# Small float32 matmuls of a hybrid decoder's mixer, regrouped over the tiles of the PE array

## Chip, cores and metric

One core of a Trainium2 chip runs the whole program. The metric is device time in microseconds, the median of the runs shown; less is better. One launch computes one layer for 512 prompt tokens and for 8 requests of 4 new tokens each, 544 tokens together.

## What is computed

The reference is one layer of a decoder in float32: a half-step feed-forward network with layer norm, a mixer, layer norm, and a second half-step network with layer norm. The change lies in the mixer. Its projection `h = x @ w_in` is split into an attention group of 8 heads (dilated windows, for the sampled tokens over a cache of 512 positions) and a delta group of 8 heads (short convolution, then the gated delta rule in chunks of 64 tokens). Cut to what matters here:

```
a     = where(strict, (kb @ k.T) * decay, 0)       # per head and chunk
t_inv = inverse(eye + a)                           # unit lower triangular
u     = t_inv @ (v * beta);   w = t_inv @ (kb * exp(gc))
intra = where(tril, (q @ k.T) * decay, 0)
def step(s, ...):                                  # 8 chunks, one after the other
    v_new = u_i - w_i @ s
    o_i   = qd_i @ s + intra_i @ v_new
    s     = s * gl_i + kd_i.T @ v_new
```

The attention of the prompt is `softmax(q k.T + bias) @ v` over causal blocks of 128 tokens. The sampled tokens have the same delta rule with one chunk of 4 tokens per request, and each request's state is updated as above.

## The kernel before

The two feed-forward networks are dense products of 128 by 128 weights with 272 token columns, kept in two float32r parts (tiles `wh`, `wl`, or `g` where weights lie there). They are outside the change. Between them stands the mixer, whose pieces are generators that yield what they want next (an engine, a rough duration, PSUM banks, tile slots). The class `Weave` runs them as lanes: it takes the lane that can start first by its own table of durations, so the numbers in each `yield` set the order in which instructions are written. Dense projection products are lanes marked `PE*`; they fill in between the small ones. PE, DVE, ACT, POOL and the DMA queue of SP each run their instructions in the order written, and wait on semaphores. The tile framework may still move an instruction by its priority, unless `together` (a chain in which each matmul is tied behind the last, the first waits for everything that the set reads or overwrites) holds it.

A float32 matmul of 64 columns is two matmul instructions in the trace, so a set of 16 calls of `mm` shows as x32. All `mm` calls have line 309. An operand on partitions 0 to 63 or 64 to 127 uses the upper or lower half of the PE array's rows, an output there its left or right columns: a 64 by 64 product occupies one of four array tiles, and one on 32 partitions a smaller tile. The pieces that the change touches, with heads in four pairs `j`, two heads `hp` in each, and chunks `u`, `p2`:

- `pair(j)`, from line 1246: k k.T and k q.T of all chunks, 32 products, into two banks `pa[hp]`.
- `inverse_load`, `solve(j)` (line 1368, one lane for each j): two sets of 32 by 32 products (`py`, `pz`) complete the inverse. Between them an ACT copy (line 1388) and after them a DVE copy (line 1398). Then 16 products for `u` (`pu`), 16 for `w` (`pw`), each set with a `yield` and an ACT copy of its own.
- `recurrence`, from line 1449: for each of 8 chunks 16 products with the state `ST` (w and q: `pb`), a DVE subtraction (line 1474), 8 products `pk` with KD, a DVE addition that makes the next state (line 1483). `chunk_out` (line 1489) then does 8 products `pi` with IN in a step of its own, two DVE multiplications (line 1502) and one DVE addition (line 1506).
- `state_sample`, line 1718: four sets of 16 products, one for each j, one bank at a time.
- `values`, line 1815: for each j and half of the prompt, two query blocks `qb`, each a set of its own behind the probabilities of its block.

In `pb`, the order of the loops is w first, then q:

```
for w, rows in ((WT, r), (QT, ro)):
    for j in range(4):
        for hp in range(2):
            mm(pb[hp][rows, j * 64:j * 64 + 64], w[j][rh, i * 64:i * 64 + 64], ST[rh, j])
```

Cached keys and values of the sampled tokens (lines 1860, 1888), biases (1774), `w_out` (2022) and the residual (2043) are loaded by SP's queue, in the order written, into tile slots that the mixer's other work frees.

Of the kernel before, what the change touches and what calls it, by code (L numbers as in the profile page):

```python
# [16 lines left out]
ALU = mybir.AluOpType  # L17
# [193 lines left out]
def trunk(ctx, tc, slots, x_prompt, x_sample, cache_k, cache_v, state_gdn, state_conv, rel_bias,  # L211
# [1003 lines left out]
    def pair(j):  # L1215
# [30 lines left out]
        for u in range(4):  # L1246
            for p2 in range(2):
                for hp in range(2):
                    c0 = u * 128 + p2 * 64
                    l = k[64 * hp:64 * hp + 64, c0:c0 + 64]  # L1250
                    o = pa[hp][64 * p2:64 * p2 + 64]
                    mm(o[:, u * 64:u * 64 + 64], l, l)
                    mm(o[:, 256 + u * 64:256 + u * 64 + 64], l, q[64 * hp:64 * hp + 64, c0:c0 + 64])
# [87 lines left out]
    XI = {}  # L1341

    def inverse_load():
# [6 lines left out]
        for i in range(4):  # L1350
            WT[i] = wj[:, i]
            XI[i] = xs_[i // 2][:, (i % 2) * 256:(i % 2) * 256 + 256]
# [15 lines left out]
    def solve(j):  # L1368

        yield "wait", "inverse loaded"  # L1370
        yield "wait", ("scaled", j)
        tt = WT[j]
        tv = tt.rearrange("p (n c) -> p n c", n=8)
        xv = XI[j].rearrange("p (n c) -> p n c", n=8)
        av = A21[j // 2][:, (j % 2) * 256:(j % 2) * 256 + 256].rearrange("p (n c) -> p n c", n=8)
        yield "PE", 0.6, 1
# [8 lines left out]
        yield "ACT", 0.7, [py]  # L1385
        for p2 in range(2):
            r = slice(64 * p2 + 32, 64 * p2 + 64)
            S.activation(xv[r], py[r, :256].rearrange("p (n c) -> p n c", n=8), AF.Copy, scale=-1.0)
        yield "PE", 0.6, 1
        pz = wv.bank()  # L1390
        for n in range(8):
# [3 lines left out]
        yield "DVE", 0.7, [pz]  # L1395
        for p2 in range(2):
            r = slice(64 * p2, 64 * p2 + 32)
            V.tensor_copy(tv[r, :, 32:64], pz[r, :256].rearrange("p (n c) -> p n c", n=8))
        yield "PE", 1.3, 1
        pu = wv.bank()  # L1400
        for u in range(4):
            for hp in range(2):
                c0 = u * 128 + hp * 64
                for p2 in range(2):
                    r = slice(64 * p2, 64 * p2 + 64)
                    mm(pu[r, c0:c0 + 64], tt[r, c0:c0 + 64], VU[r, j, c0:c0 + 64])
        yield "ACT", 0.8, [pu]
        S.copy(VU[:, j], pu)
        yield "PE", 1.3, 2
        pw = [wv.bank(), wv.bank()]  # L1410
        for u in range(4):
            for hp in range(2):
                c0 = u * 128 + hp * 64
                for p2 in range(2):
                    r = slice(64 * p2, 64 * p2 + 64)
                    mm(pw[p2][64 * hp:64 * hp + 64, u * 64:u * 64 + 64], KG[j][r, c0:c0 + 64], tt[r, c0:c0 + 64])
        w4 = WT[j].rearrange("p (u a c) -> p u a c", u=4, a=2)
        for p2 in range(2):
            yield "ACT", 0.35, [pw[p2]]
            S.copy(w4[:, :, p2], pw[p2][:, :256].rearrange("p (u c) -> p u c", u=4))  # L1420
        wv.post(("solved", j))
        yield "G", -1
# [25 lines left out]
    def recurrence():  # L1448
# [5 lines left out]
        for u in range(4):  # L1454
            ou = G(512)
            ov = ou.rearrange("p (j t e) -> p j t e", j=4, t=2)
            for p2 in range(2):
# [5 lines left out]
                for w, rows in ((WT, r), (QT, ro)):  # L1463
                    for j in range(4):
# [11 lines left out]
                yield "PE", 0.7, 2  # L1476
                pk, pi = wv.bank(), wv.bank()
                for j in range(4):
                    for hp in range(2):
                        c0 = u * 128 + hp * 64  # L1480
                        mm(pk[64 * hp:64 * hp + 64, j * 64:j * 64 + 64], KD[j][r, c0:c0 + 64], vv[r, j, hp])
# [9 lines left out]
    def chunk_out(u, p2, vv, pb, pi, ov):  # L1491
# [3 lines left out]
        yield "PE", 0.7  # L1495
        for j in range(4):
            for hp in range(2):
                c0 = u * 128 + hp * 64
                mm(pi[ro, (2 * j + hp) * 64:(2 * j + hp) * 64 + 64], IN[j][r, c0:c0 + 64], vv[r, j, hp])
# [5 lines left out]
        yield "DVE", 0.65, [pi]  # L1505
        V.tensor_tensor(ou[ro], pi[ro], ou[ro], op=ALU.add)
# [191 lines left out]
    def state_sample(kd, vn, sts):  # L1698
# [19 lines left out]
        for j in range(4):  # L1718
            r = slice(32 * j, 32 * j + 32)
            yield "PE", 0.9, 1  # L1720
            pk = wv.bank()
            for bp in range(4):
                for hp in range(2):
                    for b2 in range(2):
                        c0 = (2 * bp + hp) * 64
                        mm(pk[64 * b2:64 * b2 + 64, c0:c0 + 64], kd[r, hp * 64:hp * 64 + 64],
                           vms[bp // 2][r, 2 * (bp % 2) + b2, hp * 64:hp * 64 + 64])
            for bp in range(4):
                yield ("DVE", 0.25) if bp < 3 else ("DVE", 0.25, [pk])
                sj = sts[bp][:, 2 * j:2 * j + 2]  # L1730
                V.tensor_tensor(sj, pk[:, 128 * bp:128 * bp + 128].rearrange("p (t e) -> p t e", t=2), sj, op=ALU.add)
# [489 lines left out]
```

## Time and profile before

| | before |
|---|---|
| median of 3 runs | 1218.44 us (1215.99 to 1218.8) |
| the profiled execution | 1218.54 us, span of instructions 1216.8 us |
| PE matmul busy | 1167.1 us, 96% of the span |
| DVE busy | 905.4 us, 74% |
| ACT busy | 515.8 us, 42% |
| POOL busy | 288.0 us, 24% |
| granted PE clock, mean | 0.977 |
| chain that ended last | PE 77%, of it line 309 73%; DVE 10%; DMA 4% |

The chain names what the last instruction waited for, step by step back to the start; three quarters of it are matmuls of line 309, dense and small together. Busy shares are means over stages that are limited by different things, so the rows further below are taken stage by stage. In them a matmul's own duration includes the time that it spends behind others in the pipeline: what a set costs is read from the start of its first instruction to the start of the next group's.

### The profile page before, as it was taken

What the parts mean: (1) busy time and instruction counts of PE and PEld (TensorE: products, weight loads), DVE (VectorE), ACT (ScalarE), POOL (GpSimd) and SP (SyncE); (2) the same over time, 40 slices, a digit from 0 to 9 for tenths busy, and PEclk for the clock granted to TensorE, in tenths of its full rate; (3) what the DMA queues carried; (4) which work ended last, traced back from release to release, by engine and by line L of the source; (5) the groups of instructions that cost most, each with busy time, mean ns of one, the idle gap of its engine ahead of it and who ended that gap; (6) DMA issues with size and microseconds to landing.
All of it is one profiled execution on the core that took longest, in us unless ns stands there. A gap on an engine that the chain in (4) does not pass through costs nothing.

```text
span 1216.8 us, 25657 instructions
## 1 busy us (share of the span) xinstructions
PE 1167.1 (96%) x10375; PEld 1104.9 (91%) x10375; DVE 905.4 (74%) x1905; ACT 515.8 (42%) x1035; POOL 288.0 (24%) x363
## 2 busy tenths in 40 slices
PE   8899999999999999999999999988999999999994
PEld 7899999999999888999888675877999999999994
DVE  6878887877766587794366647688988777777767
ACT  6444444343444465433411544456444444444432
POOL 2321121111100047961314100033211111111003
PEclk8999999999999999999999999989999999999997
DMA  7553323322233222336104995321322324242112
GB/s 169 152 174 97 115 88 108 105 73 87 70 97 121 75 69 78 97 91 159 58 13 124 322 299 191 114 77 46 113 92 73 98 79 122 87 122 70 56 50 74
DMA packets 165442, 130.91 MB, mean 108 GB/s; under 512 B 31758, under 2 KB 152100, under 8 KB 165324
## 3 DMA queue, kind: packets, MB, share of 16 engines
q1 hardware_dynamic: 163852, 124.82, 34.3%
q0 software_dynamic: 1472, 4.46, 1.2%
q8 instruction: 81, 1.33, 0.5%
q14 instruction: 37, 0.30, 0.1%
HBM read 119.63 MB, written 12.33 MB: 108 GB/s over the span
## 4 chain that ended last, share of the span: by engine, by line
PE 77%; DVE 10%; DMA 4%; POOL 3%; ACT 2%; SPq 2%; issue 2%; DVEq 0%; POOLq 0%; ACTq 0%
PE bank L309 73%; PE bank L525 1%; PE bank L1866 1%; DVE wl L313 1%; DMA wf<-in_ffn_w_gate 1%; DMA wf<-in_ffn_w_up 1%; DMA g<-in_cache_attn_k 1%; PE bank L582 1%; DVE wf L1333 1%; PE bank L1812 1%; DVE tmp L1331 1%; DVE wl L923 1%; DVE lna L504 1%; DVE g L313 1%; DVE g L1001 1%
## 5 line engine op out<-in xcount | busy, mean ns | idle before, releaser
L309 PE MATMUL bank<-g,wh 128*128 128x272 f32 (+2 forms) x4864 | 943.5, 292 | 11.9 <-DVE g L313 7.0
L309 PEld LDWEIGHTS bank<-g,wh 128*128 128x128 f32 x4864 | 769.4, 190 | 24.5 <-DVE g L313 7.6
L309 PE MATMUL bank<-g,wl 128*128 128x272 f32 (+2 forms) x2432 | 703.6, 290 | 0.0
L309 PEld LDWEIGHTS bank<-g,wl 128*128 128x128 f32 x2432 | 460.8, 190 | 3.6 <-issue 3.2
L312 ACT CAST wh<-wf 128x512 fp32r<-128x512 f32 (+2 forms) x176 | 111.7, 648 | 138.8 <-PE bank L309 113.0
L712 POOL TENSOR_TENSOR wf<-wf 128x512 f32<-128x512 f32 x40 | 63.7, 1592 | 360.5 <-DVE vu L710 344.9
L313 DVE TENSOR_TENSOR wl<-wf,wh 128x512 fp32r<-128x512 f32 (+2 forms) x172 | 135.6, 799 | 11.1 <-ACT wh L312 9.0
L309 PE MATMUL bank<-g 64*64 64x64 f32 (+15 forms) x1708 | 128.7, 295 | 3.7 <-DVE g L1596 2.4
L309 PEld LDWEIGHTS bank<-g 64*64 64x64 f32 (+7 forms) x1708 | 89.8, 142 | 23.2 <-issue 10.7
L312 ACT CAST wh<-vu 128x512 fp32r<-128x512 f32 x120 | 72.3, 618 | 70.7 <-PE bank L309 70.0
L713 POOL TENSOR_TENSOR vu<-wf,vu 128x512 f32<-128x512 f32 x40 | 59.7, 1493 | 125.4 <-DVE wl L313 121.1
L313 DVE TENSOR_TENSOR wl<-vu,wh 128x512 fp32r<-128x512 f32 x120 | 81.5, 693 | 10.4 <-ACT wh L312 6.2
L313 DVE TENSOR_TENSOR g<-g 128x544 fp32r<-128x544 f32 (+1 forms) x80 | 71.4, 919 | 0.0
L312 ACT CAST wh<-g 128x512 fp32r<-128x512 f32 x64 | 38.0, 618 | 59.5 <-issue 42.0
L312 ACT CAST g<-g 128x544 fp32r<-128x544 f32 (+1 forms) x80 | 44.3, 582 | 39.6 <-DVE g L755 24.0
L313 DVE TENSOR_TENSOR wl<-g,wh 128x512 fp32r<-128x512 f32 x64 | 43.0, 693 | 24.2 <-ACT wh L312 23.4
L887 ACT COPY g<-bank 128x512 f32<-128x512 f32 (+4 forms) x64 | 30.3, 501 | 60.0 <-PE bank L309 21.6
L923 DVE TENSOR_TENSOR wl<-wf,wh 128x1024 fp32r<-128x1024 f32 x28 | 37.7, 1348 | 20.6 <-ACT wh L921 20.4
L775 DVE TENSOR_TENSOR g<-bank,g 128x272 f32<-128x272 f32 x96 | 40.0, 431 | 12.5 <-PE bank L309 12.4
L711 DVE TENSOR_TENSOR vu<-vu,wf 128x512 f32<-128x512 f32 x40 | 47.6, 1190 | 1.8
L710 DVE TENSOR_TENSOR vu<-wf 128x512 f32<-128x512 f32 x40 | 27.5, 689 | 20.9 <-DMA wf<-in_ffn_w_gate 18.3
L921 ACT CAST wh<-wf 128x1024 fp32r<-128x1024 f32 x28 | 29.2, 1050 | 28.0 <-PE bank L309 14.0
(313 smaller groups left out, 1116.7 us busy)
## 6 DMA issues: line engine op xcount, KB each, us to landing
wf<-in_ffn_w_gate SPq DMA_DIRECT2D x21, 1024.0 KB
wf<-in_ffn_w_up SPq DMA_DIRECT2D x21, 1024.0 KB
g<-in_ffn_w_down SPq DMA_DIRECT2D x64, 256.0 KB
wf<-in_w_in SPq DMA_DIRECT2D x14, 1024.0 KB
g<-in_cache_attn_k SPq DMA_DIRECT2D x32, 256.0 KB
g<-in_cache_attn_v SPq DMA_DIRECT2D x32, 256.0 KB
wf<-in_ffn_w_down SPq DMA_DIRECT2D x8, 768.0 KB
wf<-in_w_out SPq DMA_DIRECT2D x4, 1024.0 KB
```

The lines of the kernel that those rows point to most:

```text
L309: return PE.matmul(out, l, r, start=start, stop=stop, skip_group_check=again)
L312: S.copy(h, f)
L313: (GP if pool else V).tensor_tensor(l, f, h.bitcast(F32), op=ALU.subtract)
L504: V.tensor_mul(a, y, y)
L710: V.tensor_add(s1, a21, a22)
L711: V.tensor_sub(s2, s1, a11)
L712: GP.tensor_tensor(a21, a11, a21, op=ALU.subtract)
L713: GP.tensor_tensor(s4, a12, s2, op=ALU.subtract)
L775: V.tensor_add(r, pd, r)
L887: return S.copy(out, src)
L921: S.copy(h, fm)
L923: V.tensor_sub(l, fm, h.bitcast(F32))
```

## The change

Each piece keeps its products; their order and their grouping move. In `pair`, the k k.T and k q.T products no longer alternate on the same tile. `solve` takes two pairs j at once: 32 products in `py`, 32 in `pz`, with one copy of twice the width behind each, and `u` and `w` of one j form one chained set. In the recurrence, w and q products alternate, and `pi` moves out of `chunk_out` into one chained set behind `pk`; its outputs for hp = 1 go to the other half of the partitions, so that the addition in `chunk_out` becomes two of half the width. `state_sample` takes two j at once, in two banks. `values` chains both query blocks in one set, and waits for the probabilities of both.

```
@@ pair
-            for p2 in range(2):
-                for hp in range(2):
-                    ...
-                    mm(o[:, u * 64:u * 64 + 64], l, l)
-                    mm(o[:, 256 + u * 64:256 + u * 64 + 64], l, q[64 * hp:64 * hp + 64, c0:c0 + 64])
+            for i, m in enumerate((k, q)):
+                for p2 in range(2):
+                    for hp in range(2):
+                        ...
+                        mm(pa[hp][64 * p2:64 * p2 + 64, 256 * i + u * 64:256 * i + u * 64 + 64], k[rh, c0:c0 + 64], m[rh, c0:c0 + 64])
@@ solve
-    def solve(j):
+    def solve(j0):
...
-        for n in range(8):
+        for n in range(16):
             for p2 in range(2):
...
-        yield "PE", 1.3, 1
-        pu = wv.bank()
...
-        yield "PE", 1.3, 2
-        pw = [wv.bank(), wv.bank()]
...
+        for j in js:
+            tt = WT[j]
+            yield "PE", 1.5, 3
+            pu, pw = wv.bank(), [wv.bank(), wv.bank()]
+            ...
+            together([(pu[r, c0:c0 + 64], tt[r, c0:c0 + 64], VU[r, j, c0:c0 + 64]) for u, hp, p2, c0, r in at] +
+                     [(pw[p2][64 * hp:64 * hp + 64, u * 64:u * 64 + 64], KG[j][r, c0:c0 + 64], tt[r, c0:c0 + 64])
+                      for u, hp, p2, c0, r in at])
@@ recurrence
-                for w, rows in ((WT, r), (QT, ro)):
-                    for j in range(4):
+                for j in range(4):
+                    for w, rows in ((WT, r), (QT, ro)):
                         for hp in range(2):
...
-                yield "PE", 0.7, 2
+                yield "PE", 1.0, 2
                 pk, pi = wv.bank(), wv.bank()
-                for j in range(4):
-                    for hp in range(2):
-                        c0 = u * 128 + hp * 64
-                        mm(pk[64 * hp:64 * hp + 64, j * 64:j * 64 + 64], KD[j][r, c0:c0 + 64], vv[r, j, hp])
+                together([(pk[64 * hp:64 * hp + 64, j * 64:j * 64 + 64], KD[j][r, of(j, hp)], vv[r, j, hp])
+                          for j in range(4) for hp in range(2)] +
+                         [(pi[(ro, r)[hp], (2 * j + hp) * 64:(2 * j + hp) * 64 + 64], IN[j][r, of(j, hp)], vv[r, j, hp])
+                          for j in range(4) for hp in range(2)])
@@ chunk_out
-        yield "PE", 0.7
-        for j in range(4):
-            for hp in range(2):
-                c0 = u * 128 + hp * 64
-                mm(pi[ro, (2 * j + hp) * 64:(2 * j + hp) * 64 + 64], IN[j][r, c0:c0 + 64], vv[r, j, hp])
...
-        V.tensor_tensor(ou[ro], pi[ro], ou[ro], op=ALU.add)
+        for hp in range(2):
+            V.tensor_tensor(ov[ro, :, hp], pv[(ro, r)[hp], :, hp], ov[ro, :, hp], op=ALU.add)
@@ state_sample
-        for j in range(4):
-            ...
-            pk = wv.bank()
+        for js in ((0, 1), (2, 3)):
+            yield "PE", 1.0, 2
+            pk = {j: wv.bank() for j in js}
...
+                        for j in js:
+                            r = slice(32 * j, 32 * j + 32)
+                            c0 = (2 * bp + hp) * 64
+                            mm(pk[j][64 * b2:64 * b2 + 64, c0:c0 + 64], kd[r, hp * 64:hp * 64 + 64],
+                               vms[bp // 2][r, 2 * (bp % 2) + b2, hp * 64:hp * 64 + 64])
@@ values
-                    if qb == qs[0]:
-                        yield "PE", 0.2 * (qb + 1), 1
-                        po = wv.bank()
-                    else:
-                        yield "PE", 0.2 * (qb + 1)
-                    together([... for kb in range(qb + 1) for hp in (1, 0)])
-                    yield "G", -2
+                yield "PE", 0.2 * sum(qb + 1 for qb in qs), 1
+                po = wv.bank()
+                together([... for qb in qs for kb in range(qb + 1) for hp in (1, 0)])
+                yield "G", -4
```

The order of PE in the solves. Names: 32x32 with `g` alone is `py`, with `wf` is `pz` (the inverse lies in a `wf` buffer), `vu,wf` is `pu`, `wh` and `wl` are dense products. Before:

```order
L309 MATMUL bank<-g 32x32 x16
L309 MATMUL bank<-wf_7088,g 32x32 x16
L309 MATMUL bank<-g,wh 128x288 x2
L309 MATMUL bank<-g,wl 128x288
L309 MATMUL bank<-g,wh 128x288 x2
L309 MATMUL bank<-g,wl 128x288
L309 MATMUL bank<-wf_7088,g 32x32 x16
```

and with the change:

```order
L309 MATMUL bank<-g 32x32 x32
L309 MATMUL bank<-g,wh 128x288 x2
L309 MATMUL bank<-g,wl 128x288
L309 MATMUL bank<-g,wh 128x288 x2
L309 MATMUL bank<-g,wl 128x288
L309 MATMUL bank<-wf_7088,g 32x32 x32
```

Two pairs now share a set, and a set stands alone between dense products half as often.

The order of PE in the first step of the recurrence; `g 64x64` holds `pk`, `pi` and the sampled states. Before, a dense product has slipped between the first and the other seven products of `pk`, and `pi` comes five dense products later:

```order
L309 MATMUL bank<-g 64x64
L309 MATMUL bank<-g,wh 128x256
L309 MATMUL bank<-g 64x64 x7
L964 MATMUL bank<-cst,g 128x128 x4
L309 MATMUL bank<-g,wh 128x256
L309 MATMUL bank<-g,wl 128x256
L309 MATMUL bank<-g,wh 128x256 x2
L309 MATMUL bank<-g,wl 128x256
L309 MATMUL bank<-g 64x64 x8
```

With the change `pk` and `pi` are the x16, and the x32 is the first set of the sampled states, four tiles in two banks:

```order
L309 MATMUL bank<-g 64x64 x16
L1664 MATMUL bank<-cst,g 128x128
L309 MATMUL bank<-g,wh 128x288
L309 MATMUL bank<-g,wl 128x288
L309 MATMUL bank<-g 64x64 x32
```

The second set of the sampled states does not stay whole: the scheduler puts its j = 2 products first (7, then 9 behind the next `pk` and `pi`) and all 16 of j = 3 behind the fourth state set.

The order of PE at the seventh and eighth step, where cached keys are transposed on line 1866 (1857 with the change). Before:

```order
L309 MATMUL bank<-state,wf_7088 64x64 x8
L309 MATMUL bank<-state,g 64x64 x8
L1866 MATMUL bank<-cst,g 128x128 x4
L1529 MATMUL bank<-cst,g 128x128 x4
L309 MATMUL bank<-g,wl 128x256
L309 MATMUL bank<-g,wh 128x256 x2
L309 MATMUL bank<-g,wl 128x256
L309 MATMUL bank<-g 64x64 x16
```

and with the change, from the end of the seventh state set:

```order
L309 MATMUL bank<-state,g 64x64 x2
L1857 MATMUL bank<-cst,g 128x128 x4
L309 MATMUL bank<-g 64x64 x16
L309 MATMUL bank<-state,wf_7088 64x64 x2
L309 MATMUL bank<-state,g 64x64 x2
```

Here only four transposes stand between a state set and the `pk` that needs its subtraction, and nothing between `pk`, `pi` and the eighth state set.

Over the whole order of PE, the solves come in 13 stretches of small matmuls before and 8 with the change, the recurrence with the sampled states in 27 and 16, the attention of prompt and samples in 27 and 22 (a stretch ends where full-array work, a dense product or a transpose, follows). The number of matmuls is the same.

## Rows read from the trace of the kernel before

**Rows 1.** Stretches: length, busy PE, PEld, DVE, ACT, POOL, clock, DMA share, GB/s.

```profile
560.00:662.00 102.00, 101.62 (x1724) 92.38 (x1723) 53.19 (x180) 25.21 (x50) 27.57 (x50) 1.00 0.27 68
662.00:700.00 38.00, 34.98 (x311) 25.97 (x311) 26.08 (x89) 20.67 (x44) 5.33 (x9) 0.96 0.93 292
700.00:740.00 40.00, 38.42 (x344) 30.46 (x343) 21.78 (x47) 14.26 (x28) 0.71 (x4) 1.00 0.79 254
740.00:770.00 30.00, 27.77 (x210) 15.90 (x211) 23.69 (x102) 15.88 (x53) 0.00 (x0) 0.89 0.73 234
```

**Rows 2.** Timeline of PE, solves: a set of pu, a set of pw.

```profile
577.28 0.29 PE L309 MATMUL bank<-g,wl 128*128 128x288 f32 x1
577.50 1.15 PE L309 MATMUL bank<-vu,wf 64*64 64x64 f32 x32
578.58 0.50 PE L309 MATMUL bank<-g,wh 128*128 128x256 f32 x2
578.92 0.28 PE L309 MATMUL bank<-g,wl 128*128 128x256 f32 x1
579.04 0.40 PE L309 MATMUL bank<-g,wh 128*128 128x256 f32 x2
579.28 0.27 PE L309 MATMUL bank<-g,wl 128*128 128x256 f32 x1
579.48 0.69 PE L309 MATMUL bank<-wf,g 64*64 64x64 f32 x32
580.11 0.50 PE L309 MATMUL bank<-g,wh 128*128 128x256 f32 x2
```

**Rows 3.** Timeline of PE, pk (14 of 16) and pi of the first step.

```profile
604.88 0.68 PE L309 MATMUL bank<-g 64*64 64x64 f32 x14
605.48 0.66 PE L964 MATMUL bank<-cst,g 128*128 128x128 f32 x4
...
606.66 1.14 PE L309 MATMUL bank<-g 64*64 64x64 f32 x16
607.74 0.50 PE L309 MATMUL bank<-g,wh 128*128 128x256 f32 x2
```

**Rows 4.** Timeline of PE, first state set of the recurrence.

```profile
600.35 0.51 PE L309 MATMUL bank<-state,wf 64*64 64x64 f32 x10
...
600.82 0.51 PE L309 MATMUL bank<-state,g 64*64 64x64 f32 x11
601.26 0.53 PE L309 MATMUL bank<-g,wh 128*128 128x288 f32 x2
```

**Rows 5.** Groups of PE by form, 560 to 662: sampled states.

```profile
L309 PE MATMUL bank<-g 32*64 32x64 f32 x128 | 5.1, 222 | 0.0
```

**Rows 6.** Timeline of PE, a set of pair: start, length, line, operands, count.

```profile
462.18 1.30 PE L309 MATMUL bank<-g 64*64 64x64 f32 x64
463.41 0.51 PE L309 MATMUL bank<-g,wh 128*128 128x256 f32 x2
```

**Rows 7.** Groups of DVE, 560 to 670: the addition and the reduction of chunk_out.

```profile
L1506 DVE TENSOR_TENSOR g<-bank,g 64x512 f32<-64x512 f32 x8 | 5.5, 687 | 8.9 <-PE bank L309 8.8
L1514 DVE TENSOR_REDUCE oss<-g 128x8 f32<-128x512 f32 x4 | 2.7, 687 | 1.9 <-ACT g L1511 1.9
```

**Rows 8.** Timeline of DVE, subtractions of the eighth step.

```profile
660.98 0.42 DVE L1474 TENSOR_TENSOR g<-vu,bank 64x256 f32<-64x256 f32 x1 [2.58 <-PE bank L309]
...
661.89 0.42 DVE L1474 TENSOR_TENSOR g<-vu,bank 64x256 f32<-64x256 f32 x1
```

**Rows 9.** Waits of PE, 660 to 770: who for whom, us, times, longest.

```profile
PE bank L1866 <- DMA g<-in_cache_attn_k: 2.5, 2, 1.7
```

**Rows 10.** Waits of SP's queue, 430 to 860.

```profile
SPq L1860 <- PE bank L309: 54.1, 5, 44.2
```

**Rows 11.** Timeline of PE, transposes of probabilities and the waits before them.

```profile
757.85 0.55 PE L1812 MATMUL bank<-cst,g 128*128 128x128 f32 x3 [1.63 <-DVE g L1807]
758.76 0.48 PE L1812 MATMUL bank<-cst,g 128*128 128x128 f32 x1 [0.36 <-DVE sm L1797]
```

More of the change, by code (lines that the diff above doesn't have):

```diff
@@ L1351, in inverse_load @@
             WT[i] = wj[:, i]
-            XI[i] = xs_[i // 2][:, (i % 2) * 256:(i % 2) * 256 + 256]
+            XI[i] = xs_[i // 2]
+        WJ.append(wj)
         for p2 in range(2):
@@ L1384, in solve @@
                     after(i, first)
-        yield "ACT", 0.7, [py]
+        yield "ACT", 1.1, [py]
         for p2 in range(2):
             r = slice(64 * p2 + 32, 64 * p2 + 64)
-            S.activation(xv[r], py[r, :256].rearrange("p (n c) -> p n c", n=8), AF.Copy, scale=-1.0)
-        yield "PE", 0.6, 1
+            S.activation(xv[r], py[r].rearrange("p (n c) -> p n c", n=16), AF.Copy, scale=-1.0)
+        yield "PE", 1.0, 1
         pz = wv.bank()
-        for n in range(8):
+        for n in range(16):
             for p2 in range(2):
@@ L1394, in solve @@
                 mm(pz[64 * p2:64 * p2 + 32, n * 32:n * 32 + 32], xv[r, n], tv[r, n, 32:64])
-        yield "DVE", 0.7, [pz]
+        yield "DVE", 1.2, [pz]
         for p2 in range(2):
             r = slice(64 * p2, 64 * p2 + 32)
-            V.tensor_copy(tv[r, :, 32:64], pz[r, :256].rearrange("p (n c) -> p n c", n=8))
-        yield "PE", 1.3, 1
-        pu = wv.bank()
-        for u in range(4):
-            for hp in range(2):
-                c0 = u * 128 + hp * 64
[L1404 to L1408, printed above, removed]
-        yield "PE", 1.3, 2
-        pw = [wv.bank(), wv.bank()]
-        for u in range(4):
-            for hp in range(2):
-                c0 = u * 128 + hp * 64
[L1414 to L1422, printed above, removed]
+            V.tensor_copy(tv[r, :, 32:64], pz[r].rearrange("p (n c) -> p n c", n=16))
+        for j in js:
+            tt = WT[j]
+            yield "PE", 1.5, 3
+            pu, pw = wv.bank(), [wv.bank(), wv.bank()]
+            at = [(u, hp, p2, u * 128 + hp * 64, slice(64 * p2, 64 * p2 + 64)) for u in range(4) for hp in range(2) for p2 in range(2)]
+            together([(pu[r, c0:c0 + 64], tt[r, c0:c0 + 64], VU[r, j, c0:c0 + 64]) for u, hp, p2, c0, r in at] +
+                     [(pw[p2][64 * hp:64 * hp + 64, u * 64:u * 64 + 64], KG[j][r, c0:c0 + 64], tt[r, c0:c0 + 64])
+                      for u, hp, p2, c0, r in at])
+            yield "ACT", 0.6, [pu]
+            S.copy(VU[:, j], pu)
+            w4 = WT[j].rearrange("p (u a c) -> p u a c", u=4, a=2)
+            for p2 in range(2):
+                yield "ACT", 0.35, [pw[p2]]
+                S.copy(w4[:, :, p2], pw[p2][:, :256].rearrange("p (u c) -> p u c", u=4))
+            wv.post(("solved", j))
+            yield "G", -1
     def keep(kind, i):
@@ L1724, in state_sample @@
                     for b2 in range(2):
[L1725 to L1731, printed above, removed]
+                        for j in js:
+                            r = slice(32 * j, 32 * j + 32)
+                            c0 = (2 * bp + hp) * 64
+                            mm(pk[j][64 * b2:64 * b2 + 64, c0:c0 + 64], kd[r, hp * 64:hp * 64 + 64],
+                               vms[bp // 2][r, 2 * (bp % 2) + b2, hp * 64:hp * 64 + 64])
+            for j in js:
+                for bp in range(4):
+                    yield ("DVE", 0.25) if bp < 3 else ("DVE", 0.25, [pk[j]])
+                    sj = sts[bp][:, 2 * j:2 * j + 2]
+                    V.tensor_tensor(sj, pk[j][:, 128 * bp:128 * bp + 128].rearrange("p (t e) -> p t e", t=2), sj, op=ALU.add)
         for b in range(8):
@@ L2108, in trunk @@
     wv.add(gates(), recurrence())
-    for j in range(4):
+    for j in (0, 2):
         wv.add(solve(j))
```

35 lines of the change are left out of this document (15 added, 20 removed).

## The prediction

> **What bounds the kernel now.** I read the windows first: is PE the limit in the stages that the change touches, or something beside it? From 560 to 662 us, where solves, recurrence and sampled states run among dense products, PE is busy for 101.62 of 102 us at full clock, DVE for 53.19, and DMA moves little (0.27) [rows 1]. A microsecond taken from PE there is a microsecond off the time, as long as no wait takes its place. From 662 to 740 us, where attention begins, PE still has 73.4 of 78 us, but DMA is at 0.93 and then 0.79; from 740 to 770 the clock is 0.89 and PE idles for 2.2 us [rows 1]. So the question is whether what is saved ahead of 662 us survives the next hundred. The dense products of the two networks behind and ahead are untouched.
>
> Next the timeline of PE, set by set, since a matmul's own duration includes its place in the pipeline. I take differences of starts. A set of `pw`, which goes round four tiles, holds 32 instructions and takes 0.63 us; one of `pu`, the same number on two tiles, takes 1.08 [rows 2]. The last instruction needs some 0.12 us to leave whatever the pace, so the paces are (0.63 - 0.12) / 32 = 16 ns and (1.08 - 0.12) / 32 = 30 ns. `pi`, which sits on one tile, has 16 in 1.08 us [rows 3], 60 ns each. Four tiles, two, one: 16, 30, 60 ns; the price of a product goes with how many tiles its neighbours leave idle. The 0.12 is chosen as what makes the three stand in that ratio.
>
> A set also has an edge. The `wl` product ahead of `pu` takes 0.22 us from its start to the set's, where 0.13 would do (two `wh` of 256 columns take 0.24 between dense products, so 288 columns some 0.135 each); the two `wh` after a set take 0.34 instead of 0.24 [rows 2]. So an edge is 0.09 before, 0.12 of tail and 0.10 behind: 0.31 us for each stretch of small matmuls that stands by itself.
>
> **The change, part by part.** All savings are PE time.
>
> - *State sets.* Today w runs on two tiles, then q on the other two: 0.91 us for 32 instructions [rows 4]. Alternating, they are as `pw`: 0.63. 8 x 0.28 = 2.2 us.
> - *`pi` beside `pk`.* `pk` has two tiles already, 14 instructions in 0.60 us [rows 3], and stays. `pi` goes from one tile to two: 16 x (60 - 30) ns = 0.48 us a step, 8 x 0.48 = 3.8 us. That is the largest single term apart from edges.
> - *Sampled states.* 128 instructions cost 5.1 us, four sets of nearly 1.3 [rows 5]. Two sets' worth on four tiles is 64 instructions, as in a set of `pair`, 1.23 us [rows 6]: 2.55 - 1.23 = 1.3 us. The second two sets stay apart by j in the order, so I give them nothing (bounds 0 and another 1.3).
> - *Edges.* Solves fall from 13 stretches to 8 and the recurrence with sampled states from 27 to 16: 16 x 0.31 = 5.0 us. Low bound: if the 0.12 of tail were hidden, 16 x 0.19 = 3.0.
> - *Values.* 5 stretches fewer in the attention, 1.5 us at most; the bounds are 0 and 1.5, and I take 1.5, because PE has 92% and more of these stretches as well [rows 1].
> - *`pair`.* A set is x64 in 1.23 us, (1.23 - 0.12) / 64 = 17 ns [rows 6]: four tiles' pace already. Nothing.
> - *ACT and DVE.* The solve's copies are half as many and twice as wide. The addition of `chunk_out`, 687 ns for 64 by 512 [rows 7], becomes two of 256 columns, each as the 0.42 us of the 64 by 256 subtraction [rows 8]: 0.15 us more, 8 times, 1.2 us on an engine with 49 us free in that stretch [rows 1]. I cost both at nothing; if that cover failed, they would cost 1.2.
>
> Sum: 2.2 + 3.8 + 1.3 + 5.0 + 1.5 = 13.8 us.
>
> Against it stand two new waits. The first is at the end of the recurrence. A step's chain is state set, subtraction, `pk`, addition, next state set, and what hides DVE is the dense work put between. In step 8 of today the second subtraction starts at 661.89 and ends 0.42 later, at 662.31 [rows 8], about 1.4 us behind its state set. In the new order the seventh step has only four transposes there, 0.5 us, and between `pk` with `pi` and the eighth state set nothing. So PE waits there for about 1.4 - 0.5 = 0.9 us, and again for the addition that makes the state, whose price I take as the two 0.42 [rows 8], 0.8 us: 1.7 us together. Ends: 0, if DVE is free at once and PE behind, and 1.7 + 2 x 0.69 = 3.1, if an addition or reduction of `chunk_out` [rows 7] stands ahead in DVE's queue both times. Behind the waiting `pk` on PE are only the eighth step and then attention, which needs its end in any case.
>
> The second is cached keys. PE waits for them 2.5 us today, in 2 waits [rows 9]. PE comes some 12 us earlier; SP's queue has been held by PE's own progress (54.1 us of waits on line 309 [rows 10]), so most loads move forward too, but into a stretch in which DMA is already at 0.93 [rows 1]. I charge the same 2.5 us again (ends 0 and 6, the latter worked out below).
>
> 13.8 - 1.7 - 2.5 = 9.6 us. The profiled execution took 1218.54 us, 0.1 from the median of the runs, so 1218.5 - 9.6 = **1208.9 us**. With edges at their low bound 1211; with neither wait, 1204.7; with both sampled sets at four tiles as well, 1203.4. The case's own range is 1204 to 1212.
>
> The pace of 16 ns is itself what one may doubt. Thirty-two instructions in 0.63 us are below 20 ns each, even with the tail counted in [rows 2]. The Trainium skill, page "TensorE: Matmul & The Clock Gate", Part 1, says that start-to-start never drops below about 25 ns however few the columns; by it a set of 32 would take 32 x 25 ns and a tail, 0.92 us, as the state set has today, and four tiles would bring nothing over two. The trace disagrees with it: 0.63.
>
> **Rivals.**
>
> *The loads set the end of the stage (B).* From 662 to 740 us DMA is busy for 0.93 x 38 + 0.79 x 40 = 66.9 us. At the 0.93 that it reaches it would need 72 of the 78 us [rows 1]. If loads started no earlier than now, attention could gain at most 6 us, whatever PE saved before: 1212.5. A PE that waits more also has more of what makes the granted clock 0.96 over 38 us, 1.5 us [rows 1]: up to 1214.0. For it: DMA's shares, and PE's waits for keys [rows 9]. Against: the loads wait for slots that PE frees [rows 10], so they move with it.
>
> *The joined value sets wait (C, slower).* Each of the 8 value sets now needs the probabilities of the second block before the first block's products may run; in the order the transposes of the last probabilities stand directly ahead. Where PE reaches these transposes too early it waits today for the softmax, 1.63 us for its multiplication and 0.36 for its sum [rows 11], 2.0 together. If every set met that, 16 us: 1218.5 - 13.8 + 4.2 + 16 = 1224.9. It decides from (9.6 + 3.7) / 8 = 1.7 us a set. For it: DVE is at 23.69 of 30 us from 740 to 770 [rows 1]. Against: the first block's products are short, so that joining gives up little cover.
>
> *Only the edges come (D).* If a set's pace were bound by something other than the tiles (reads of the operands, or two row halves that write one bank), state sets, `pi` and sampled states would gain nothing, 7.3 us less: 1216.2. Against: `pu`, `pw` and `pi` stand in the ratio of their tiles [rows 2, 3], but no row shows `pk` and `pi` in one set. A smaller case of it is a floor at which four tiles cost what two do: then 2.2 + 1.3 fall away, 1212.4.
>
> *Better (E).* Neither wait costs anything, and fewer idle moments bring the clock of 0.89 [rows 1] up: 30 us at 0.96 in its place gain 2 us. 1208.9 - 1.7 - 2.5 - 2 = 1202.7.
>
> **How the numbers follow.** Some 0.3%, 3.7 us, is what a measurement of this kernel can tell from no change: faster means below 1214.8, slower above 1222.1. Chances: forecast 0.60; loads 0.20; value sets 0.08; only edges 0.05, and the floor alone 0.02; better 0.05. Faster takes in the forecast, the better case, the floor, and all but a little of the loads: 0.85. Same: the upper end of loads, only edges, a mild form of the value sets: 0.09. Slower: the rest of the value sets, 0.06. The range reaches from 1204.0, the low end of the forecast, to 1215.5, over the loads' case and half of the way into that of the edges; outside lie the value sets, the rest of the edges, and most of the better case, under 2 in 10.
>
> **What would show it.** In the profile after, a state set should take about 0.6 us where 0.91 stood, `pk` with `pi` about 32 x 30 ns + 0.12 = 1.1, and a sampled set of 64 1.2. The recurrence should be over some 11 us sooner than now. Before the seventh `pk` and the eighth state set there should be waits on DVE of about 1 us each; in attention PE's waits on key loads should be near 5 us. If the sets have the paces but the stage from 662 us on gives back more than 5 us to DMA, it was the loads; if transposes or values on PE wait for the softmax 8 times by some 2 us, it was the value sets; if the sets keep today's durations, the reason is wrong at its root. No wait at the seventh step would mean that DVE had less in its queue than I read.

## The result, and the profile after

The changed kernel takes 1205.05 us (median of 4 runs, 1201.47 to 1206.83); its ratio to the kernel before, which came to 1217.66 us in the same comparison, is 0.9886 (0.9868 to 0.9905). That is 13.9 us less, where 9.6 were forecast: the direction was right, the gain was half again as large, and 0.9886 of 1217.66, 1203.8, lies just below the range. A second set of runs gave 0.9888 (0.9865 to 0.9911). The profiled execution, 1206.83 us, is the slowest of its four.

The stages of the changed kernel, some 14 us earlier than those of [rows 1] (window: length, busy PE, PEld, DVE, ACT, POOL, clock, DMA share, GB/s):

```profile
560.00:648.00 88.00, 85.51 (x1675) 79.36 (x1674) 55.27 (x172) 24.32 (x47) 27.05 (x48) 0.98 0.33 82
648.00:686.00 38.00, 35.02 (x304) 26.80 (x302) 24.00 (x80) 18.29 (x40) 6.55 (x11) 1.00 0.82 252
686.00:726.00 40.00, 38.14 (x367) 30.87 (x366) 20.88 (x51) 15.56 (x28) 0.35 (x2) 0.96 0.80 265
726.00:756.00 30.00, 26.49 (x196) 14.61 (x195) 22.13 (x86) 13.31 (x39) 0.36 (x2) 0.90 0.62 205
```

In the window of the solves and the recurrence PE was idle for 0.4 us before [rows 1]; now it is for 88.00 - 85.51 = 2.5, so the small products gave more than the time shows. The timeline of PE shows both (start, length, operands, count, in brackets the wait ahead):

```profile
595.21 0.27 PE L309 MATMUL bank<-state,wf 64*64 64x64 f32 x2
595.22 0.27 PE L309 MATMUL bank<-state,g 64*64 64x64 f32 x2
...
595.68 0.23 PE L309 MATMUL bank<-state,g 64*64 64x64 f32 x2
595.83 0.50 PE L309 MATMUL bank<-g,wh 128*128 128x256 f32 x2
...
599.45 1.15 PE L309 MATMUL bank<-g 64*64 64x64 f32 x32 [0.16 <-DVE g L1467]
601.21 0.33 PE L1664 MATMUL bank<-cst,g 128*128 128x128 f32 x1 [0.62 <-DVE g L1659]
...
601.73 1.16 PE L309 MATMUL bank<-g 32*64 32x64 f32 x64
602.82 0.53 PE L309 MATMUL bank<-g,wh 128*128 128x288 f32 x2
...
640.06 0.66 PE L1857 MATMUL bank<-cst,g 128*128 128x128 f32 x4
641.46 1.15 PE L309 MATMUL bank<-g 64*64 64x64 f32 x32 [0.75 <-DVE g L1467]
643.54 0.27 PE L309 MATMUL bank<-state,wf 64*64 64x64 f32 x2 [0.93 <-DVE da L504]
```

The state set runs from 595.21 to 595.83, 0.62 us where it was 0.91 [rows 4]. `pk` with `pi` is the x32 at 599.45; less the 0.62 that the next instruction waits, it takes 601.21 - 599.45 - 0.62 = 1.14 us, where `pk` and `pi` took more than 0.60 and 1.08 [rows 3]. The 64 sampled products take 1.09, half of the old 5.1 being 2.55. All 128 stand in the groups by form at 4.0, where 5.1 stood [rows 5]:

```profile
L309 PE MATMUL bank<-g 32*64 32x64 f32 x128 | 4.0, 221 | 0.0
```

A set of `pair` takes 463.23 - 462.14 = 1.09 us where 1.23 stood [rows 6], so `pair`, for which the prediction gave nothing, brought some 0.6 in four sets:

```profile
462.14 1.16 PE L309 MATMUL bank<-g 64*64 64x64 f32 x64
463.23 0.51 PE L309 MATMUL bank<-g,wh 128*128 128x256 f32 x2
```

The seventh `pk` waits 0.75 for its subtraction, and the eighth state set 0.93. The profile puts this second wait down to `da` L504, the last DVE instruction to start before it; what the set needs is the state from the addition (L1478), which ends at 643.39. DVE's timeline there:

```profile
639.74 0.69 DVE L1506 TENSOR_REDUCE oss<-g 128x8 f32<-128x512 f32 x1 [0.70 <-ACT g L1503]
640.47 0.17 DVE L1508 TENSOR_TENSOR oss<-oss,rq 128x8 f32<-128x8 f32 x1
640.66 0.74 DVE L1467 TENSOR_TENSOR g<-vu,bank 64x256 f32<-64x256 f32 x2
...
642.97 0.42 DVE L1478 TENSOR_TENSOR state<-bank,state 128x256 f32<-128x256 f32 x1
```

The eighth state set starts 16.4 us sooner than before (643.54 against 659.98), where some 11 were forecast; 44 dense products that stood ahead of it now stand behind it, which is worth some 5.5 us of that.

From 640 to 770 us, that is at the end of the recurrence and in attention, PE's waits of 0.7 us and more are these (who for whom, us, times, longest):

```profile
PE bank L1806 <- DVE g L1801: 2.6, 5, 1.0
PE bank L1857 <- DMA g<-in_cache_attn_k: 2.2, 3, 1.3
PE bank L309 <- DVE sm L1790: 1.7, 1, 1.7
PE bank L309 <- DVE da L504: 0.9, 1, 0.9
PE bank L309 <- DMA g<-in_cache_attn_v: 0.8, 1, 0.8
PE bank L309 <- ACT g L887: 0.8, 1, 0.8
PE bank L309 <- DVE g L1467: 0.7, 1, 0.7
```

The waits on cached keys are 2.2 us, 0.3 less than before [rows 9]; a wait of 0.8 on cached values is new. Those on the softmax (L1801, L1790) are 4.3 where 2.0 stood [rows 11]. The waits on ACT's copy (L887) fell from 1.8 to 0.8; the larger of them before was this one:

```profile
PE bank L1866 <- ACT g L887: 1.6, 1, 1.6
```

So the sets gave nearly what they should, the tight steps cost what they should, and the loads cost 0.5 us more than before instead of the 2.5 that were charged.

**Work and stalls.** From the start of the first `pair` set to a product early in the second network, some 2800 matmuls before the end, each kernel runs the same 4024 matmul instructions. This stretch in the kernel before, and then in the changed one (columns as above):

```profile
462.20:847.30 385.10, 361.87 (x4024) 313.35 (x4024) 263.15 (x749) 153.09 (x341) 129.53 (x237) 0.96 0.44 129
```

```profile
462.20:835.60 373.40, 346.70 (x4024) 302.54 (x4024) 262.27 (x753) 151.62 (x337) 130.24 (x237) 0.97 0.45 133
```

PE is idle for 23.2 us of it before and 26.7 after. The granted clock is at half (1.2 of 2.4 GHz) in pieces of 3.413 us; each costs up to half of that, 1.71. There are 8 in this stretch before, 7 after. One of them begins at 644.4 us in the changed kernel, and a `wl` product of 288 columns takes 0.24 us there from its start to the next, where [rows 2] gave some 0.13:

```profile
644.62 0.44 PE L309 MATMUL bank<-g,wl 128*128 128x288 f32 x1
644.86 0.44 PE L309 MATMUL bank<-g,wh 128*128 128x288 f32 x1
```

Busy time less half of each piece is PE's work at full clock: 361.87 - 13.65 = 348.22 and 346.70 - 11.95 = 334.75. **The work fell by 13.5 us, the idle time rose by 3.5, the clock gave back 1.7.** Together that is 11.7 us, the whole difference between the two profiled executions (1218.54 and 1206.83). The experiments are read in the same three numbers.

### The profile page after: what moved, and what is told of

Same layout as the page of the kernel before. It is cut to its first block, busy times and chain, and to the rows that moved or that the text cites. A ratio compares the mean times of both kernels' runs of the same rounds, so it can differ in the third digit from the quotient of the medians.

```text
span 1204.9 us, 25663 instructions
## 1 busy us (share of the span) xinstructions
PE 1152.3 (96%) x10375; PEld 1094.4 (91%) x10375; DVE 905.8 (75%) x1909; ACT 514.6 (43%) x1031; POOL 288.8 (24%) x363
## 4 chain that ended last, share of the span: by engine, by line
PE 72%; DVE 14%; DMA 5%; issue 3%; POOL 3%; ACT 2%; SPq 0%; DVEq 0%; ACTq 0%; POOLq 0%
PE bank L309 68%; DVE wl L313 2%; DVE g L313 2%; PE bank L525 1%; DMA wf<-in_w_in 1%; DVE wl L923 1%; DMA wf<-in_ffn_w_up 1%; DVE wf L1332 1%; PE bank L582 1%; DVE vu L711 1%; DVE tmp L1330 1%; DMA wf<-in_w_out 1%; DMA g<-in_x_prompt 1%; PE bank L1857 1%; DVE g L1001 0%
## 5 line engine op out<-in xcount | busy, mean ns | idle before, releaser
L309 PE MATMUL bank<-g 64*64 64x64 f32 (+17 forms) x1708 | 118.0, 292 | 5.8 <-DVE g L1588 1.8
L309 PEld LDWEIGHTS bank<-g 64*64 64x64 f32 (+7 forms) x1708 | 81.9, 140 | 24.2 <-issue 10.0
L887 ACT COPY g<-bank 128x512 f32<-128x512 f32 (+4 forms) x64 | 30.8, 498 | 55.9 <-PE bank L1857 23.6
```

Source lines behind the costliest of these rows:

```text
L309: return PE.matmul(out, l, r, start=start, stop=stop, skip_group_check=again)
L887: return S.copy(out, src)
```

## Experiments

Ratios are to the kernel before in the same set of runs, with 95% intervals. Profiles: the 4024 instructions of each kernel, idle, pieces and work as above. Where many pieces lie, work is underestimated, since not all that runs in a piece loses its half: e11, which differs from e10 and from the changed kernel in order alone and has the most pieces, shows 3.6 and 4.0 us less work, 0.4 and 0.7 us for each piece more. Differences in work between rows with unlike numbers of pieces are sure only to that.

| run | ratio | stretch us | idle us | pieces | work us |
|---|---|---|---|---|---|
| before | 1 | 385.1 | 23.2 | 8 | 348.2 |
| changed | 0.9886 | 373.4 | 26.7 | 7 | 334.8 |
| changed again (e5) | 0.9888 (0.9865 to 0.9911) | 372.5 | 26.2 | 7 | 334.3 |
| e1 state order undone | 0.9914 (0.9901 to 0.9928) | 373.3 | 24.7 | 7 | 336.7 |
| e2 pi on one tile | 0.9926 (0.9914 to 0.9939) | 374.4 | 19.6 | 11 | 336.1 |
| e3 solves undone | 1.0018 (1.0005 to 1.0032) | 388.2 | 32.8 | 13 | 333.2 |
| e4 values alone | 0.9978 (0.9969 to 0.9987) | 380.3 | 22.2 | 6 | 347.9 |
| e6 held | 0.9944 (0.9923 to 0.9966) | 378.1 | 23.5 | 13 | 332.5 |
| e7 held, samples tied | 0.9933 (0.9913 to 0.9953) | 375.7 | 27.0 | 9 | 333.3 |
| e8 pi apart | 0.9897 (0.9872 to 0.9921) | 371.4 | 20.3 | 8 | 337.5 |
| e9 solves, pair, values alone | 0.9970 (0.9953 to 0.9987) | 382.4 | 23.2 | 11 | 340.4 |
| e10 one number, state set | 0.9845 (0.9825 to 0.9865) | 361.8 | 22.3 | 3 | 334.4 |
| e11 one number, u and w | 0.9958 (0.9943 to 0.9972) | 381.2 | 28.2 | 13 | 330.8 |
| e12 samples tied | 0.9908 (0.9892 to 0.9924) | 371.5 | 27.2 | 6 | 334.0 |

**e1.** The order of the state set undone:

```
-                for j in range(4):
-                    for w, rows in ((WT, r), (QT, ro)):
+                for w, rows in ((WT, r), (QT, ro)):
+                    for j in range(4):
```

> The changed kernel with one part undone: in the eight state sets all w products come first again, then all q products, so that only two array tiles are at work at a time; nothing else moves. Theory (a set costs what its idle tiles cost, and PE is the bound of the recurrence): a state set goes from about 0.62 us back to 0.91, and the time rises by 8 x 0.29 = 2.3 us over the changed kernel's (some 1204 to 1206, so about 1207). Rival 1 (what is won in the mixer is given back in attention): the set's duration goes back, the time does not, under 0.8 us. Rival 2 (a floor on the time between starts, so that four tiles cost what two do): set and time stay as in the changed kernel.

Its first state set and the dense product behind it:

```profile
595.37 0.51 PE L309 MATMUL bank<-state,wf 64*64 64x64 f32 x10
...
596.27 0.50 PE L309 MATMUL bank<-g,wh 128*128 128x256 f32 x2
```

0.90 us again, and 0.28% of 1217, 3.4 us, above the changed kernel, though the two intervals touch (work: 1.9 more; 2.3 were expected). The floor falls: 32 instructions in 0.62 us on four tiles and in 0.90 on two.

**e2.** `pi` stays chained behind `pk`, on one tile:

```
-                         [(pi[(ro, r)[hp], (2 * j + hp) * 64:(2 * j + hp) * 64 + 64], IN[j][r, of(j, hp)], vv[r, j, hp])
+                         [(pi[ro, (2 * j + hp) * 64:(2 * j + hp) * 64 + 64], IN[j][r, of(j, hp)], vv[r, j, hp])
...
-        for hp in range(2):
-            V.tensor_tensor(ov[ro, :, hp], pv[(ro, r)[hp], :, hp], ov[ro, :, hp], op=ALU.add)
+        V.tensor_tensor(ou[ro], pi[ro], ou[ro], op=ALU.add)
```

> The changed kernel with pi still chained behind pk in one set, but all of pi on one array tile as before the change, and one addition of 64 by 512 in place of two of half the width. It parts the price of the tiles from that of the edges. Theory (tiles): a joint set takes 16 x 30 + 16 x 60 ns + 0.12 = 1.56 us instead of 1.1, 0.48 more, 8 times: 3.8 us over the changed kernel. Rival 1 (only the edge of the set was won): the joint set takes the same 1.1 us and the time is the same. Rival 2 (given back behind): the set is 0.48 us longer, the time rises by less than half of 3.8.

```profile
600.35 1.61 PE L309 MATMUL bank<-g 64*64 64x64 f32 x32
602.12 0.33 PE L1662 MATMUL bank<-cst,g 128*128 128x128 f32 x1 [0.16 <-DVE g L1657]
```

602.12 - 600.35 - 0.16 = 1.61 us, near the 1.56 foretold and 0.47 more than with two tiles. The time rose by 0.40%, 4.9 us, but not by this alone: the profile has 7.1 us less idle time and four more pieces of half clock. The work rose by 1.3, or by 3 to 4 if the underestimate for four more pieces is allowed for; 3.8 - 1.2 = 2.6 was to be expected, since in this order the second set of the sampled states stayed whole, which gives back 1.2.

**e3.** The solves as before the change:

```
-    def solve(j0):
+    def solve(j):
...
-    for j in (0, 2):
+    for j in range(4):
         wv.add(solve(j))
```

> The changed kernel with the solves as before: one pair j at a time, 16 products in each of its sets, u and w apart. Theory (edges alone): five stretches of small matmuls more at 0.31 us each, 1.6 us over the changed kernel. Rival (the solves are worth more than their edges: in the profile of the changed kernel the first state set starts 5.1 us sooner than before, of which only 1.0 was there ahead of the solves): 4 us over the changed kernel. If neither, because dense products only changed sides of the first state set, the time rises by 0 to 1 us.

Neither the 1.6 us of the theory nor the 4 of the rival came out: the whole gain is gone, and more. Yet the work is no higher. Idle time and half clock are. The stretch, the largest waits and one of them:

```profile
460.70:848.90 388.20, 355.43 (x4024) 311.60 (x4024) 264.59 (x760) 152.86 (x340) 130.14 (x237) 0.94 0.43 128
```

```profile
PE bank L1931 <- DVE g L1923: 5.7, 1, 5.7
PE bank L1863 <- DMA g<-in_cache_attn_k: 4.6, 4, 1.9
```

```profile
748.29 1.09 PE L1931 MATMUL bank<-cst,g 128*128 128x128 f32 x4 [5.72 <-DVE g L1923]
```

L1931 transposes the sampled tokens' probabilities, L1923 scales them. In this order they stand on PE with a single transpose between them and their scores, so that PE waits for the whole softmax. No line of that code differs: what the edit can have moved there is the order, which is worked out from the table of durations. Whether this is it, or the solves hold a price of their own, e9 to e11 ask.

**e4.** The kernel before with the value sets joined:

```
+                yield "PE", 0.2 * sum(qb + 1 for qb in qs), 1
+                po = wv.bank()
+                together([(po[64 * hp:64 * hp + 64, qb * 128:qb * 128 + 128], VT[kb][:, 128 * j + 64 * hp:128 * j + 64 * hp + 64],
...
+                          for qb in qs for kb in range(qb + 1) for hp in (1, 0)])
```

> The kernel before with one part of the change alone: both query blocks of a value set in one chain, behind the probabilities of both. Theory: the edges of some three stretches, 3 x 0.31 = 0.9 us less than the kernel before, if nothing waits. Rival (the joined sets wait for the last softmax): up to 2 us for each of 8 sets, shown by PE's waits on the probabilities, and a time some us above the kernel before.

0.22%, 2.7 us, faster, where 0.9 were expected; the profile shows some 0.3 us of work, 1.0 of idle time and two pieces of half clock less, so most of that is not the edges. The waits on probabilities did not come.

**e5.** The changed kernel once more.

> The changed kernel itself, once more beside the others of this set, to narrow its interval (0.9886, 0.9868 to 0.9905) and to see how many stretches at half clock another profile of it shows. Theory (terms of PE's sets land in full, the charged waits on cached keys do not, and the half-clock stretches vary from run to run): the ratio stays in 0.987 to 0.990. Rival (the four runs were lucky): 0.990 to 0.992, the forecast of 1208.9 would be right to a microsecond or two.

As the theory had it; the idle time, the work and the pieces agree to half a microsecond with the first profile.

**e6, e7, e12.** Dense products held behind the set that they are written after (in e6 and e7), and the sets of the sampled states chained (in e7 and e12):

```
+                    if last_st[0] is not None and k == 2 * part:
+                        after(m, last_st[0])
...
-                            mm(pk[j][64 * b2:64 * b2 + 64, c0:c0 + 64], kd[r, hp * 64:hp * 64 + 64],
+            together([(pk[j][64 * b2:64 * b2 + 64, (2 * bp + hp) * 64:(2 * bp + hp) * 64 + 64],
```

> The changed kernel with the dense products of the recurrence held where they are written, behind the state set or the set of pk and pi ahead of them, so that about 12 of them stand in each gap and the seventh and eighth step are no longer without cover. Theory (the two waits of 0.75 and 0.93 us there are real, and the half-clock stretch of 3.4 us that starts at 644.5, right behind them, is their doing): the waits go, and with them the stretch: 1.7 to 3.4 us less than the changed kernel beside it. Rival 1 (the waits only hand their time to attention, which waits for keys or the softmax instead): under 0.8 us. Rival 2 (12 dense products, 1.5 us, are too few to cover the DVE): short waits at every step and a time the same or longer.

> As the held kernel beside it, and the 32 products of each set of the sampled states chained, so that the second set (j = 2 and 3) stays whole on four tiles. Theory: the second set goes from about 2.4 us in pieces to about 1.2, and one or two edges of 0.31 fall away: 1.3 to 1.8 us less than the held kernel. Rival (what is won here is given back behind): under 0.6 us.

> The changed kernel with the sampled states' sets chained, so that the second set stays whole, and nothing held. Theory: 1.2 us less of PE's work than in the changed kernel (as the run with pi on one tile showed, where that set stayed whole by itself: 2.4 us for all 128 products, 3.6 in the changed kernel), and 0.3 us for an edge: 1.5 us faster if stalls stay as they are. Rival (the order behind it moves and decides): a time off by 3 us or more in either direction, with the work as foretold.

e6 came out wrong in sign: it is 6 to 7 us slower than the changed kernel beside it (e5). With 12 dense products in every gap PE still waits 2.3 us for the subtractions, in two waits, and the clock is at half in 13 pieces instead of 7. This is nearest to its second rival (too little cover), and since the waits did not go, the run does not show what they are worth. e7 is 1.3 us below e6, as was expected of it, but the intervals overlap; it is 5 us slower than the changed kernel too. In e12 the products of the sampled states cost 2.3 us in place of 4.0, as foretold, and the work is 0.8 us less than the changed kernel's, but the 1.5 us of time did not come: 0.9908 is no faster, and the two intervals overlap.

**e8.** `pi` back in a set of its own, on one tile:

```
+        yield "PE", 0.7
+        for j in range(4):
+            for hp in range(2):
+                c0 = u * 128 + hp * 64
+                mm(pi[ro, (2 * j + hp) * 64:(2 * j + hp) * 64 + 64], IN[j][r, c0:c0 + 64], vv[r, j, hp])
```

> The changed kernel with pi back in chunk_out as a set of its own on one tile. Against the run with pi on one tile inside the joint set it prices the edge of a set: six stretches more. Theory (0.31 us an edge): 1.9 us above that run (0.9926 of the kernel before), some 0.994 to 0.9945, and 5.7 us above the changed kernel. Rival 1 (an edge costs nothing once dense products stand on both sides): the same as that run. Rival 2 (pi apart gives the tight steps their cover back): faster than that run.

The time is that of rival 2, 0.9897, below the 0.9926 of e2. The reason is not shown to be its cover: against e2 the work is 1.4 us higher and the idle time 0.7, and three pieces of half clock fewer make up for both. Against the changed kernel the work is 2.7 us higher and the idle time 6.4 lower. Of that, 1.9 us are waits on DVE in the recurrence (0.5 us from 560 to 650, where the changed kernel has 2.4 to 648): there `pi` apart does cover DVE. The other 4.5 lie in other stages.

**e9.** Solves, `pair` and values regrouped, the rest (state order, `pi`, sampled states) as before the change:

```
-                for j in range(4):
-                    for w, rows in ((WT, r), (QT, ro)):
+                for w, rows in ((WT, r), (QT, ro)):
+                    for j in range(4):
...
-        for js in ((0, 1), (2, 3)):
-            yield "PE", 1.0, 2
+        for j in range(4):
```

> The changed kernel with only the regrouped solves, pair sets and value sets left: state sets, pi and sampled states as before the change. The run with the solves alone undone lost the whole gain (1.0018), though PE's work at full clock, from the first pair set to the second network, came out as low there as in the changed kernel; what rose was idle time and half clock, by 15 us. Theory A (solves are worth their sets and edges, some 2.2 us, and that run lost the rest because another order of the attention stage stalls more): 2.2 + 0.9 of the values, some 3 us below the kernel before, ratio near 0.9975, unless its own order stalls more or less. Theory B (joining the solves is itself worth 14 us, by a wait that it takes away): a ratio near 0.988 here too.

0.9970, the number of theory A: the joined solves are not worth 14 us. Its reason fits less well. The work is 7.8 us below that of the kernel before, some 6 if the three more pieces of half clock are allowed for, where A gave 3.1, and the clock takes 5.1 back. In e3, on the other hand, undoing the solves left the work as it was. How the saving divides among solves, `pair` and values stays open.

**e10 and e11.** One number each; the same instructions in another order.

```
-                yield "PE", 1.4, 2
+                yield "PE", 0.9, 2
                 pb = [wv.bank(), wv.bank()]
```

and

```
-            yield "PE", 1.5, 3
+            yield "PE", 1.2, 3
             pu, pw = wv.bank(), [wv.bank(), wv.bank()]
```

> The changed kernel with one number altered: the duration that the order's table gives a state set, 1.4 before and 0.9 here. The same instructions, in another order. Theory (the order of the attention stage decides some us of idle time and half clock, apart from any part of the change): PE's work at full clock the same within 1 us, idle and half clock together different by 3 us or more, and the time with them. Rival (the order hardly matters, a part's time is its work): the time of the changed kernel within 1.5 us.

> As the run with another number for the state set, with the number of the joined set of u and w altered instead, 1.5 before and 1.2 here. Theory and rival as there; in this order attention is interleaved with the last steps of the recurrence much more than in the changed kernel, so the stalls may come out anywhere within some 10 us of it.

The stretch of e10 and of e11:

```profile
460.80:822.60 361.80, 339.52 (x4024) 297.59 (x4024) 264.75 (x750) 152.62 (x340) 128.97 (x237) 0.99 0.46 137
```

```profile
460.80:842.00 381.20, 353.01 (x4023) 308.18 (x4024) 265.55 (x756) 151.91 (x333) 130.17 (x237) 0.94 0.44 130
```

19 us lie between them (15 between the medians of their runs), and neither changes a product. e10 has 4.4 us less idle time than the changed kernel and 3 pieces of half clock instead of 7, at the same work: the theory. e11 has 1.5 more and 13; its work, 4.0 lower by this measure, is not within the 1 us that the theory gave, which is put down to the many pieces. e10 takes 1197.51 us (1196.42 to 1200.5) and beats both kernels. PE's waits in it from 640 to 770 us are these and no others; those on the softmax have all but gone:

```profile
PE bank L1857 <- DMA g<-in_cache_attn_k: 1.2, 2, 1.0
PE bank L1857 <- DVE g L888: 1.0, 1, 1.0
PE bank L309 <- DVE g L888: 1.0, 1, 1.0
PE bank L309 <- ACT g L887: 0.8, 1, 0.8
PE bank L309 <- DVE sm L1800: 0.3, 1, 0.3
```

## Why the prediction was right, and where it was wrong

**The sum was right.** 13.8 us of PE's time were forecast, and 13.5 (13.9 in the second profile) less work were found. By terms: state sets 0.29 us each instead of 0.28 (e1); `pi` 0.47 a step instead of 0.48 (e2); sampled states 1.1 instead of 1.3, the second set in pieces as foretold (e12: whole, it would have given 1.7 more). State sets, `pi` and sampled states make 7.2 of the 13.5; the 6.3 that are left are edges, values and `pair` together, for which 6.5 were forecast (of them 0.6 in `pair`, where nothing was). They are the part with the weakest proof: no run parts the edges from the order cleanly, e4 shows 0.3 us of work for the values where 1.5 were taken, and e3 and e9 disagree about the solves.

**The step that failed is the charge for waits.** "I charge the same 2.5 us again" for cached keys: the waits on them were 2.2 us against 2.5, and with the 0.8 on cached values the loads added 0.5. The loads of keys did move forward: the first is issued at 625.0 us instead of 637.2, the last at 709.9 instead of 717.7. The 1.7 us of the seventh and eighth step came, 0.75 and 0.93, but the size is partly luck. The prediction took the 1.4 us from a step in which a multiplication stands between the two subtractions. In the changed kernel they stand together, and a reduction of `chunk_out` (L1506) stands ahead, which the prediction had only at its upper end; from the end of the state set to the end of the subtractions it is 1.34 us all the same (640.06 to 641.40). Not foreseen were 0.8 us of waits in the first step and 2.3 us more on the softmax, which stood in the prediction only as a rival, while other waits fell; and one piece of half clock less, of which the text spoke only in two of its rivals. Charged 4.2, measured 3.5 - 1.7 = 1.8. With a sum 0.3 too high this makes the 2.1 us by which the profiled executions differ more than forecast (11.7 for 9.6). The other 2.2, up to 13.9, lie between these executions and the runs that have no profile; the runs of one kernel scatter by some 5 us, and the cause in each stays open.

**The deeper fault is the form of that charge.** It went through the waits that the new order would add at two places, and let the rest of the order stand. But the order of the attention stage is computed from the same table of durations, so that any edit upstream deals it anew. For nearly the same work, idle time and clock together came to 27.4 us (e10: 22.3 + 5.1) and to 50.4 (e11: 28.2 + 22.2), with 38.6 in the changed kernel and 36.9 before; a range of 1204 to 1215.5 was far too narrow for that, and that the changed kernel came out within 2 us of the stalls of before was not something that the rows could tell: to that extent it is luck that the forecast came as near as it did. The chance of slower, 0.06, rested on the value sets; e3, which lacks one part of the change, came out 0.18% slower than the kernel before, with no more work than the changed kernel; that the order did it is argued from e9 to e11, not shown.

**Rivals.** The loads did not set the end of the stage: DMA has 0.82 and 0.80 in the two windows after, against 0.93 and 0.79 [rows 1], and the waits on loads grew by 0.5 us only. The value sets did not cost 1.7 us each. The case that only edges come fell with e1 and e2, its smaller form, the floor, with e1. The better case gives 1202.7 and 1204.7 is the forecast with neither wait, both close to what came, but not for their reason: the waits of the tight steps are there, and the clock of the fourth window is 0.90 where 0.89 stood.

## What to carry to other kernels

Price small matmuls by start-to-start times of sets and count how many array tiles each set keeps at work; here that sum held to half a microsecond, its single terms less well. Where a planner's numbers set the order, an edit also deals a new order to everything behind it: compare kernels by work, idle time and half clock over the same instructions before a gain or a loss is put down to the edit. Then move the numbers alone: here one of them gained a further 5 us (e10), another lost 9 (e11).

## What was not expected of the hardware

The granted clock decided as much as the products did: 3 to 13 pieces of 3.4 us at 1.2 GHz for the same work. In the 14 profiles these pieces lie in 83 stretches, one to four in a row; ahead of all but two (e9 at 633.2 us, e11 at 613.6) PE had stood idle for 1.0 us or more in the few microseconds before. In the changed kernel one starts at 644.4 us, behind the waits of 0.75 and 0.93, one at 692.2, behind a wait of 1.68 on the softmax, and two at 750.2, behind this:

```profile
747.24 0.66 PE L1806 MATMUL bank<-cst,g 128*128 128x128 f32 x4 [0.78 <-DVE g L1801]
748.32 0.55 PE L1806 MATMUL bank<-cst,g 128*128 128x128 f32 x3 [0.42 <-DVE g L1801]
749.90 0.85 PE L1806 MATMUL bank<-cst,g 128*128 128x128 f32 x4 [1.04 <-DVE g L1801]
```

A wait of a microsecond or two can thus cost 1.7 us more behind it. The Trainium skill, page "TensorE: Matmul & The Clock Gate", section "HAM oscillation — how this bites in real kernels", says that a PE which waits for its data is throttled again and begins the next work cold. The rows agree, though the waits of its example are 3 to 5 us and those here much shorter. Not every wait has such a piece behind it: the waits of 0.16 and 0.62 us in the first step have none. In e8, where the waits of the tight steps are gone, so is the piece behind them: the clock is 1.00 from 560 to 650 us; in e12 one wait of 0.86 us stands there, and no piece. That speaks for the waits, but these runs differ in more than the wait, and what decides was not settled. Nor was it tried to change the kernel before by a number alone, which would show what the order is worth without the change.
